# Another load order and a side-by-side start of block 1 in a matmul with logsumexp

## The chip, the core and the metric

The kernel runs on one core of one Trainium2 chip. The metric is the device time of one execution in microseconds; lower is better. The kernel before has a median of 441.1 us over 3 runs (440.34 to 441.67).

## The reference

```python
def setup_inputs():
    m, k, n = 1024, 4096, 4096
    return {"a": np.random.randn(m, k).astype(np.float32),
            "b": np.random.randn(k, n).astype(np.float32)}

def reference(a, b):
    x = np.matmul(a, b)
    return special.logsumexp(x, axis=-1).astype(np.float32)
```

The output is one number for each of the 1024 rows of A.

## The kernel before

**Tiling.** The rows of A form 8 tiles (`MT`, index `m`) of 128 rows, K is cut into 32 tiles (`KT`) of 128, and the columns of B into 8 blocks (`NB`, index `nb`) of 512. A and B lie in HBM as float32; the DMAs cast them to float16 on their way into SBUF. The row tiles go in four pairs or quads `q` (`m` = 2q and 2q+1), and the k tiles in 16 pairs (`KP`, index `i`), in four groups `g` of four pairs.

**Two ways to multiply.** Block 0 of the columns is done by plain matmuls (`plain`, L184; 128x512, 8 x 32 = 256 of them). Blocks 1 to 7 are done, quad by quad, by Strassen's scheme: seven products `m1` to `m7` of 16 matmuls of 128x256 each (all issued at L314) in place of eight. Their left operands are `aT` (A transposed), the sums `s1`, `s2`, `s5`, and `aT` after two differences were written into it in place; the right ones are raw blocks of B and `T1`, `T4`, `T6` and two in-place sums (`do_t1` to `do_t3`, on VectorE). A quad keeps two PSUM tiles `r0` = (c11, c12) and `r1` = (c21, c22). ScalarE copies intermediate states out (`s`, L359 and L364; `x`, L397 and L399), VectorE forms the sums (L78, L81) and the negated row maxima (`lse_max`, L84), and ScalarE the exponentials with their sums (`lse_exp`, L89); the exponentials of one quad are held in `pending` and issued by `flush` in the next.

**Load and transpose phase** (L139 to L281). K is taken in four chunks `kc` of 1024. A's part of a chunk comes as 8 DMAs (`load_a`, L155), one for each row tile, B's part of block 0 as 4 DMAs (L256), all from GpSimd's queue, each 256 KB as it lands. Each A load is staged in one of 12 slots, and a slot is used again for a later load. The slots lie in the memory that `T1`, `T4` and `T6` (tile `tb`) take later:

```python
    stg_slots = tb.rearrange("p t (i j) n -> p (t i) (j n)", j=4)
    NSLOT = 3 * KP // 4
        slot = stg_slots[:, (kc * MT + m) % NSLOT]
```

`transpose_group` (L160) transposes a staged tile with 8 matmuls (L166) into one of two PSUM tiles `tps_0`, `tps_1` in turn; groups of even number are copied to `aT` by VectorE (L177), odd ones by ScalarE (L179). The lists `arrivals` and `back` set the order: after the transposes of one arrival, TensorE does the work (`behind`) of the arrival two places earlier: the plain matmuls that became possible, and the sums of A (`a_sums_early`). Row tiles 6 and 7 have no PSUM tile in this phase, since six accumulators and the two `tps` take all eight banks; their plain matmuls come after the phase (L279 to L282), in the accumulators `acc_l`. Then VectorE prepares block 1 (L283 to L291), and the loop over blocks starts (L301).

**Warm-up matmuls.** `warm(n)` (L240) issues `n` matmuls of 128x512 on a zeroed region into the accumulator of row tile 5: ten before the loads, and three after each arrival until three A tiles of the first chunk have been through `behind`, 31 in all. The zeroed region is the last staging slot:

```python
    zeros = stg_slots[:, NSLOT - 1]
    nc.vector.memset(zeros[:, 0:FD], 0.0)
    warm(10)
```

**What sets the order.** `tc.manual_schedule()` keeps each engine's instructions in the order of the text. The waits between engines and DMAs are put in by the framework: each instruction waits for what stands before it in the text and writes what it reads, or reads or writes what it writes. In the loop of before, all loads of a chunk stand ahead of all transposes and warm-ups of that chunk, and behind those of the chunk before.

**PSUM and small buffers.** All PSUM tiles share one ring of 8 banks: six accumulators, two `tps`, then `acc_l` (the banks of row tiles 0 and 1), block 1's quad 0 (those of 2 and 3), quad 1 (4 and 5), quad 2 (`tps`), and so on. `s` and `x` have one buffer each. B's tiles `bt` have eight, four to a block.

Of the kernel before, what the change touches and what calls it, by code (L numbers as in the profile page):

```python
# [13 lines left out]
def kernel(  # L14
# [6 lines left out]
    nc = tc.nc  # L21
    P = 128
    FD = 512
    H = FD // 2
# [52 lines left out]
    def add(o, x, y):  # L77
        nc.vector.tensor_tensor(out=o, in0=x, in1=y, op=ALU.add)  # L78
# [71 lines left out]
        psum_pool.tile([P, 2 * FD], f16, name=f"tps_{h}", tag="ps") for h in range(2)  # L150
    ]

    def load_a(kc, m):
        slot = stg_slots[:, (kc * MT + m) % NSLOT]
        nc.gpsimd.dma_start(out=slot, in_=a_m[m, :, ts(kc, SC)])  # L155
        stg[kc, m] = slot

# [2 lines left out]
    def transpose_group(kc, m):  # L160
        src = stg.pop((kc, m))
        n = count[0]
        count[0] += 1
        pst = tps[n % 2]
        for j in range(JT):
            nc.tensor.matmul(  # L166
                pst[:, ts(j, P)],
                src[:, ts(j, P)],
                ident,
                is_transpose=True,  # L170
                start=(j == 0),
                stop=(j == JT - 1),
            )
        dst = aT[:, ts(kc, GI), :, m // 2, m % 2, :]
        v = pst.rearrange("p (i t c) -> p i t c", i=GI, t=2)
        if n % 2 == 0:
            nc.vector.tensor_copy(out=dst, in_=v)  # L177
        else:
            nc.scalar.copy(out=dst, in_=v)  # L179
# [3 lines left out]
    def plain(pt, i, kp, m):  # L183
        nc.tensor.matmul(  # L184
            pt,
            aT[:, i, kp, m // 2, m % 2, :],
            blk0.raw[i // GI][:, i % GI, kp, :],
            start=(done[m] == 0),
            stop=(done[m] == KT - 1),
        )  # L190
        done[m] += 1

    def a_sums_early(kc, q):
        r = ts(kc, GI)
        a11, a12 = aT[:, r, 0, q, 0, :], aT[:, r, 1, q, 0, :]
        a21, a22 = aT[:, r, 0, q, 1, :], aT[:, r, 1, q, 1, :]
        add(s1[:, r, q], a11, a22)
        add(s2[:, r, q], a21, a22)
        add(s5[:, r, q], a11, a12)

    def a_sums_late(q):
        a11, a12 = aT[:, :, 0, q, 0, :], aT[:, :, 1, q, 0, :]
        a21, a22 = aT[:, :, 0, q, 1, :], aT[:, :, 1, q, 1, :]
        sub(a21, a21, a11)
        sub(a12, a12, a22)

    def first_max(m):
        lse_max(acc[m // 2][m % 2], m, 0)
        lse_exp(acc[m // 2][m % 2], m, 0)


    arrivals = []
    for n, m in enumerate((0, 6, 1, 7, 2, 3, 4, 5)):
        arrivals.append(("a", m))
        if n < GI:
            arrivals.append(("b", n))

    have_a, have_b = [[] for _ in range(KC)], [[] for _ in range(KC)]

    def behind(kc, what, x):  # L220

        if what == "a":
            have_a[kc].append(x)
            todo = [(k, x) for k in have_b[kc]]
            if x % 2 == 1:
                a_sums_early(kc, x // 2)
        else:
            ks = [kc * JT + 2 * x, kc * JT + 2 * x + 1]
            have_b[kc].extend(ks)
            todo = [(k, m) for k in ks for m in have_a[kc]]  # L230
        for k, m in todo:
            if m < MT - 2:
                plain(acc[m // 2][m % 2], k // 2, k % 2, m)
        if kc == KC - 1 and what == "a" and x in (3, 4, 5):
            for m in {3: (0, 1), 4: (2,), 5: (3, 4, 5)}[x]:
                first_max(m)
            if x > 3:
                a_sums_late(x - 4)

    def warm(n):  # L240
        for _ in range(n):
            nc.tensor.matmul(acc[2][1], zeros[:, 0:P], zeros[:, 0:FD], start=True, stop=True)  # L242

    zeros = stg_slots[:, NSLOT - 1]
    nc.vector.memset(zeros[:, 0:FD], 0.0)  # L245
    warm(10)
    back = []
    for kc in range(KC):
        bt = bt_pool.tile([P, GI, 2, FD], f16, name=f"b_0_{kc}", tag="bt")
        blk0.raw.append(bt)  # L250
        for what, x in arrivals:
            if what == "a":
                load_a(kc, x)
            else:
                r0 = (kc * JT + 2 * x) * P
                nc.gpsimd.dma_start(  # L256
                    out=bt[:, x],
                    in_=b[r0 : r0 + 2 * P, ts(0, FD)].rearrange("(t p) n -> p t n", p=P),
                )
            if kc == 0 and x == 0 and what == "a":  # L260
                make_identity(nc, ident)
                nc.gpsimd.memset(negmax, 3.0e38)
                nc.gpsimd.memset(tsum, 0.0)
        for what, x in arrivals:
            if what == "a":
                transpose_group(kc, x)
            if kc == 0 and len(have_a[0]) < 3:
                warm(3)
            if len(back) == 2:
                behind(*back.pop(0))  # L270
            back.append((kc, what, x))
    while back:
        behind(*back.pop(0))

    blk = Block(1)
    for g in range(G):
        blk.raw.append(load_b(1, g))

    last = acc_tiles("l")  # L279
    for m in range(MT - 2, MT):  # L280
        for k in range(KT):  # L281
            plain(last[m % 2], k // 2, k % 2, m)  # L282
    for g in range(G):  # L283
        if g == G - 1:
            for m in range(MT - 2, MT):
                lse_max(last[m % 2], m, 0)
                lse_exp(last[m % 2], m, 0)
        for f in (blk.do_t1, blk.do_t6, blk.do_t4, blk.do_t7, blk.do_t3):
            f(g)
    for q in range(2, MP):  # L290
        a_sums_late(q)  # L291


    pending = []
# [6 lines left out]
    for nb in range(1, NB):  # L301
        nxt = None
        if nb + 1 < NB:
            nxt = Block(nb + 1)
            for g in range(G):
                nxt.raw.append(load_b(nb + 1, g))
        for q in range(MP):
            r0, r1 = acc_tiles(f"{nb}_{q}")
            c11, c12 = r0[:, 0:H], r0[:, H:FD]
            c21, c22 = r1[:, 0:H], r1[:, H:FD]  # L310

# [8 lines left out]
                        skip_group_check=True,  # L320
                    )

            first, tail = nb == 1 and q == 0, nxt is not None and q == MP - 1
            final = nxt is None and q == MP - 1

            s = fix_pool.tile([P, 3, H], f32, name=f"s_{nb}_{q}", tag="s")
            x = fix_pool.tile([P, 2, H], f32, name=f"x_{nb}_{q}", tag="x")

            def m1(c, **k):
                product(c, lambda i: s1[:, i, q], lambda i: T1[:, i], **k)  # L330

            def m5(c, **k):
                product(c, lambda i: s5[:, i, q], lambda i: blk.b(i, 1, 1), **k)

            def m2(c, **k):
                product(c, lambda i: s2[:, i, q], lambda i: blk.b(i, 0, 0), **k)

            def m6(c, **k):
                product(c, lambda i: aT[:, i, 0, q, 1], lambda i: T6[:, i], **k)

            def m7(c, **k):
                product(c, lambda i: aT[:, i, 1, q, 0], lambda i: blk.b(i, 1, 0), **k)
# [4 lines left out]
            def m4(c, **k):  # L347
                product(c, lambda i: aT[:, i, 1, q, 1], lambda i: T4[:, i], **k)

            if first:  # L350
                for g in range(G):
                    m1(c11, start=True, g=g)
                    m5(c12, g=g)
                    m2(c21, start=True, g=g)
                    m6(c22, g=g)
            else:
                m1(c11, start=True)
                m5(c12)
            nc.scalar.copy(out=s[:, 0:2], in_=r0.rearrange("p (h n) -> p h n", h=2))  # L359
            flush()  # L360
            if not first:
                m2(c21, start=True)
# [2 lines left out]
            if tail:  # L365
                for g in range(G):
                    nxt.do_t1(g)
            add(s[:, 2], s[:, 2], s[:, 1])
            sub(s[:, 0], s[:, 2], s[:, 0])
            if final:  # L370

                z = psum_pool.tile([P, FD], f32, name="z", tag="ps")[:, 0:H]
                y = fix_pool.tile([P, H], f32, name="y")
                m3(c12)
                nc.scalar.copy(out=x[:, 0], in_=c12)
                nc.scalar.copy(out=y, in_=c11)
                m4(c21)
                nc.scalar.copy(out=x[:, 1], in_=c21)
                m7(z, start=True)
                sub(x[:, 0], x[:, 0], s[:, 0])  # L380
                sub(y, y, s[:, 2])
                lse_max(c12, 2 * q, nb)
                lse_exp(c12, 2 * q, nb)
                add(c22, c22, x[:, 0])
                lse_max(r1, 2 * q + 1, nb)
                lse_exp(r1, 2 * q + 1, nb)
                add(y, y, x[:, 1])
                add(z, z, y)
                lse_max(z, 2 * q, NB)
                lse_exp(z, 2 * q, NB)  # L390
                continue
# [12 lines left out]
            for h in range(2):  # L404
                lse_max(rows[h], 2 * q + h, nb)
                pending.append(lambda h=h, q=q, nb=nb, rows=rows: lse_exp(rows[h], 2 * q + h, nb))
            if tail:
                for f in (nxt.do_t4, nxt.do_t7, nxt.do_t3):
                    for g in range(G):
                        f(g)  # L410
# [43 lines left out]
```

## Time and profile before

| | |
|---|---|
| median of 3 runs | 441.1 us |
| the profiled execution | 441.06 us, of which the span from first to last instruction is 438.6 us |
| TensorE busy | 427.2 us (97%), 3679 matmuls |
| VectorE, ScalarE, GpSimd busy | 228.1 us (52%), 109.7 us (25%), 54.1 us (12%) |
| mean granted TensorE clock | 0.997 |
| read from HBM | 83.89 MB |
| A loads / loads of B's block 0 | 32 / 16 DMAs of 256 KB, some 9.5 us from issue to landing |
| loads of B's blocks 1 to 7 | 4 DMAs of 1024 KB each |

The times of the profile count from the first instruction. In the answers below, a line of the timeline has the start, the length, the engine, the line of the kernel, the operation, what it writes and reads, the count, and in brackets how long the engine was idle before it and what released it. Instructions of one kind in a row are merged to one line. A matmul's length reaches over the next one's start, so the pace of matmuls is read from the starts.

### The profile page before, as it was taken

The page shows a single profiled execution, that of the slowest core. Times are in us where ns is not written, and L with a number is a line of the kernel's source. Part 1 is how long each engine was busy: PE and PEld are TensorE (multiplying, and loading weights), DVE is VectorE, ACT ScalarE, POOL GpSimd, SP SyncE. Part 2 cuts the span into 40 slices and gives each one's busy share as a digit, 9 for nine tenths or more (in the row PEclk, how much of TensorE's full clock was granted, in tenths as well). Part 3 has the DMA queues.
Part 4 walks back from the last instruction along what each step waited for, and adds up shares of the span by engine and source line. Part 5 has one row for each costly group of instructions (what it writes and reads, how often), then busy time and mean ns, then how long its engine had stood idle before and what let it go on. Part 6 is the DMA issues. An engine that isn't in the chain of part 4 may idle for free.

```text
span 438.6 us, 8381 instructions
## 1 busy us (share of the span) xinstructions
PE 427.2 (97%) x3679; PEld 348.9 (80%) x3679; DVE 228.1 (52%) x425; ACT 109.7 (25%) x262; POOL 54.1 (12%) x84
## 2 busy tenths in 40 slices
PE   7999999999999999999999999999999999999995
PEld 3555554488888888888888888888888888888884
DVE  0434449973358632693348732693347722693224
ACT  2122324012222212222222122222222122222223
POOL 7435440200003000300003000300003000000000
PEclk9999999999999999999999999999999999999998
DMA  8999999998008920298008920199007930000000
GB/s 128 208 207 207 209 208 207 207 207 136 2 0 137 207 44 0 31 207 149 1 0 130 207 50 1 24 207 157 0 1 122 208 57 0 2 1 1 1 1 0
DMA packets 38260, 42.48 MB, mean 97 GB/s; under 512 B 1360, under 2 KB 34128, under 8 KB 38224
## 3 DMA queue, kind: packets, MB, share of 16 engines
q0 software_dynamic: 38080, 41.95, 56.9%
q8 instruction: 28, 0.46, 0.4%
q14 instruction: 8, 0.07, 0.1%
q1 hardware_dynamic: 144, 0.00, 0.0%
HBM read 83.89 MB, written 0.00 MB: 191 GB/s over the span
## 4 chain that ended last, share of the span: by engine, by line
PE 85%; DMA 11%; POOL 2%; issue 1%; DVE 1%; ACT 0%; POOLq 0%; DVEq 0%
DMA tb<-in_a_dram 6%; DMA b_3_540<-in_b_dram 2%; DMA b_2_395<-in_b_dram 2%; PE acc_0_0_2460 L314 2%; PE acc_0_0_1916 L314 2%; PE acc_0_0_4084 L314 2%; PE acc_0_0_3004 L314 2%; PE acc_0_0_1372 L314 2%; PE acc_0_0_3548 L314 2%; PE acc_1_0_3677 L314 2%; PE acc_3_0_2847 L314 2%; PE acc_2_0_1086 L314 2%; PE acc_3_0_3391 L314 2%; PE acc_2_0_3262 L314 2%; PE acc_1_0_2589 L314 2%; PE acc_3_0_1759 L314 2%
## 5 line engine op out<-in xcount | busy, mean ns | idle before, releaser
L314 PEld LDWEIGHTS <-aT 128*128 128x128 f16 x1792 | 175.2, 98 | 24.3 <-issue 4.2
L314 PEld LDWEIGHTS <-s_69 128*128 128x128 f16 x448 | 43.8, 98 | 5.3
L314 PEld LDWEIGHTS <-s_70 128*128 128x128 f16 x448 | 43.8, 98 | 5.1
L314 PEld LDWEIGHTS <-s_71 128*128 128x128 f16 x448 | 43.8, 98 | 5.1
L184 PEld LDWEIGHTS <-aT 128*128 128x128 f16 x256 | 24.0, 98 | 24.6
L177 DVE COPY aT<-tps_84 128x1024 f16<-128x1024 f16 x16 | 11.1, 692 | 39.8 <-PE tps_84 L166 39.8
L179 ACT COPY aT<-tps_85 128x1024 f16<-128x1024 f16 x16 | 16.2, 1012 | 50.8 <-PE tps_85 L166 50.8
L166 PEld LDWEIGHTS <-tb 128*128 128x128 f16 x256 | 16.2, 99 | 14.7 <-DMA tb<-in_a_dram 11.1
L155 POOL DMA_DIRECT2D tb<-in_a_dram x32 | 17.7, 555 | 26.0 <-PE tps_84 L166 11.6
L166 PE MATMUL tps_85<-ident,tb 128*128 128x128 f16 x128 | 9.9, 220 | 3.8 <-DMA tb<-in_a_dram 3.6
L166 PE MATMUL tps_84<-ident,tb 128*128 128x128 f16 x128 | 10.1, 224 | 1.0 <-DMA tb<-in_a_dram 1.0
L242 PE MATMUL acc_1_83<-tb 128*128 128x512 f16 x31 | 9.6, 461 | 1.2 <-DVE tb L245 1.2
L81 DVE TENSOR_TENSOR aT<-aT 128x2048 f16<-128x2048 f16 x8 | 9.3, 1222 | 0.0
L242 PEld LDWEIGHTS <-tb 128*128 128x128 f16 x31 | 3.2, 112 | 4.9 <-issue 2.2
L78 DVE TENSOR_TENSOR s_69<-aT 128x512 f16<-128x512 f16 x16 | 6.7, 418 | 0.1
L78 DVE TENSOR_TENSOR s_71<-aT 128x512 f16<-128x512 f16 x16 | 6.7, 420 | 0.0
L78 DVE TENSOR_TENSOR s_70<-aT 128x512 f16<-128x512 f16 x16 | 6.7, 419 | 0.0
L104 POOL DMA_DIRECT2D b_0_2452<-in_b_dram x1 | 0.9, 878 | 46.1 <-PE acc_3_0_2303 L314 46.1
L104 POOL DMA_DIRECT2D b_0_3540<-in_b_dram x1 | 0.9, 878 | 46.1 <-PE acc_3_0_3391 L314 46.1
L104 POOL DMA_DIRECT2D b_0_1908<-in_b_dram x1 | 0.9, 878 | 46.0 <-PE acc_3_0_1759 L314 46.0
L104 POOL DMA_DIRECT2D b_0_2996<-in_b_dram x1 | 0.9, 878 | 46.0 <-PE acc_3_0_2847 L314 46.0
L104 POOL DMA_DIRECT2D b_0_1364<-in_b_dram x1 | 0.9, 873 | 43.7 <-PE acc_3_0_1215 L314 43.7
(1034 smaller groups left out, 844.7 us busy)
## 6 DMA issues: line engine op xcount, KB each, us to landing
tb<-in_a_dram POOLq DMA_DIRECT2D x32, 256.0 KB, 9.5
b_0_97<-in_b_dram POOLq DMA_DIRECT2D x4, 256.0 KB, 7.1
b_1_250<-in_b_dram POOLq DMA_DIRECT2D x4, 256.0 KB, 9.2
b_2_395<-in_b_dram POOLq DMA_DIRECT2D x4, 256.0 KB, 9.3
b_3_540<-in_b_dram POOLq DMA_DIRECT2D x4, 256.0 KB, 9.3
b_0_720<-in_b_dram POOLq DMA_DIRECT2D x1, 1024.0 KB, 13.6
b_1_722<-in_b_dram POOLq DMA_DIRECT2D x1, 1024.0 KB, 17.4
b_2_724<-in_b_dram POOLq DMA_DIRECT2D x1, 1024.0 KB, 21.2
```

The costliest lines, as they stand in the source:

```text
L78: nc.vector.tensor_tensor(out=o, in0=x, in1=y, op=ALU.add)
L81: nc.vector.tensor_tensor(out=o, in0=x, in1=y, op=ALU.subtract)
L104: nc.gpsimd.dma_start(out=flat[:, h * step : (h + 1) * step], in_=rows[:, g * 2 * GI + h * step : g * 2 * GI + (h + 1) * step, ts(nb, FD)],)
L155: nc.gpsimd.dma_start(out=slot, in_=a_m[m, :, ts(kc, SC)])
L166: nc.tensor.matmul(pst[:, ts(j, P)], src[:, ts(j, P)], ident, is_transpose=True, start=(j == 0), stop=(j == JT - 1),)
L177: nc.vector.tensor_copy(out=dst, in_=v)
L179: nc.scalar.copy(out=dst, in_=v)
L184: nc.tensor.matmul(pt, aT[:, i, kp, m // 2, m % 2, :], blk0.raw[i // GI][:, i % GI, kp, :], start=(done[m] == 0), stop=(done[m] == KT - 1),)
L242: nc.tensor.matmul(acc[2][1], zeros[:, 0:P], zeros[:, 0:FD], start=True, stop=True)
L314: nc.tensor.matmul(c, lhs(i), rhs(i), start=(start and i == 0), stop=(i == KP - 1), skip_group_check=True,)
```

## The change

- **Load order.** `arrivals` becomes one list over all chunks: for each chunk the A tiles 0 to 5 with the four pieces of B's block 0 between them, and behind the last chunk the A tiles 6 and 7 of all four chunks. The slot of a load is its number in this list modulo 12.
- **Where the loads stand in the text.** Ahead of each arrival's transposes, as many loads are issued as there are slots: an A load while fewer than 12 A loads are ahead of the transposes, a B load always. Block 1's loads follow the last of them.
- **Plain matmuls of tiles 6 and 7** run as these tiles arrive; `acc_l` is taken when the first of them does.
- **Sums of A.** `a_sums_late` is done by chunk for quads 0 to 2; those of quad 3, early and late, move behind quad 1 of block 1. `first_max` of row tiles 0 to 5 moves with the arrivals; that of 6 and 7 moves from the fourth to the third group of block 1's preparation.
- **Quads 0 and 1 of block 1** are issued side by side: for each group `g`, the pieces of `m1`, `m5`, `m2`, `m6` of quad 0 and then of quad 1. The other three products follow quad by quad.
- **Small buffers.** `s` and `x` become one tile of four parts, in which `x` takes parts 1 and 3; the copy of `r0` is called `e` and lies in parts 0 and 1 of `s`, but in a tile of its own in quad 1 of block 1 and in the last quad (where it also takes over from `y`).

```diff
+    loads = [0]
     def load_a(kc, m):
-        slot = stg_slots[:, (kc * MT + m) % NSLOT]
+        slot = stg_slots[:, loads[0] % NSLOT]
+        loads[0] += 1
...
-    for n, m in enumerate((0, 6, 1, 7, 2, 3, 4, 5)):
-        arrivals.append(("a", m))
-        if n < GI:
-            arrivals.append(("b", n))
+    for kc in range(KC):
+        for m in range(MT - 2):
+            arrivals.append((kc, "a", m))
+            if m < GI:
+                arrivals.append((kc, "b", m))
+    for kc in range(KC):
+        for m in range(MT - 2, MT):
+            arrivals.append((kc, "a", m))
...
         for k, m in todo:
-            if m < MT - 2:
-                plain(acc[m // 2][m % 2], k // 2, k % 2, m)
-        if kc == KC - 1 and what == "a" and x in (3, 4, 5):
-            for m in {3: (0, 1), 4: (2,), 5: (3, 4, 5)}[x]:
-                first_max(m)
-            if x > 3:
-                a_sums_late(x - 4)
+            if m == MT - 2 and k == 0:
+                acc.append(acc_tiles("l"))
+            plain(acc[m // 2][m % 2], k // 2, k % 2, m)
+        if what == "a" and x % 2 == 1 and x < MT - 2:
+            a_sums_early(ts(kc, GI), x // 2)
+        if kc > 0 and what == "a" and x in (3, 4, 5):
+            a_sums_late(ts(kc - 1, GI), x - 3)
+        if kc == KC - 1 and what == "a" and x in (4, 5):
+            first_max(2 * x - 8)
+            first_max(2 * x - 7)
+        if what == "a" and x >= MT - 2:
+            n = 2 * kc + x - (MT - 2)
+            if n < 2:
+                first_max(4 + n)
+            elif n < 5:
+                a_sums_late(ts(KC - 1, GI), n - 2)
...
     zeros = stg_slots[:, NSLOT - 1]
     nc.vector.memset(zeros[:, 0:FD], 0.0)
     warm(10)
...
+    coming = list(arrivals)
     back = []
...
+    for kc, what, x in arrivals:
+        while coming and (coming[0][1] == "b" or loads[0] < count[0] + NSLOT):
+            load(*coming.pop(0))
+            if loads[0] == 1 and not blk0.raw:
                 make_identity(nc, ident)
                 nc.gpsimd.memset(negmax, 3.0e38)
                 nc.gpsimd.memset(tsum, 0.0)
...
+        if not coming and not blk.raw:
+            for g in range(G):
+                blk.raw.append(load_b(1, g))
+        if what == "a":
+            transpose_group(kc, x)
+        if kc == 0 and len(have_a[0]) < 3:
+            warm(3)
+        if len(back) == 2:
+            behind(*back.pop(0))
+        back.append((kc, what, x))
...
-    for m in range(MT - 2, MT):
-        for k in range(KT):
-            plain(last[m % 2], k // 2, k % 2, m)
-    for g in range(G):
-        if g == G - 1:
+        if g == 2:
             for m in range(MT - 2, MT):
-                lse_max(last[m % 2], m, 0)
-                lse_exp(last[m % 2], m, 0)
+                first_max(m)
...
-            s = fix_pool.tile([P, 3, H], f32, name=f"s_{nb}_{q}", tag="s")
-            x = fix_pool.tile([P, 2, H], f32, name=f"x_{nb}_{q}", tag="x")
+            s = fix_pool.tile([P, 4, H], f32, name=f"s_{nb}_{q}", tag="s")
+            x, e = s[:, 1::2], s[:, 0:2]
+            if final or (first and q == 1):
+                e = fix_pool.tile([P, 2, H], f32, name=f"e_{nb}_{q}", tag="e")
...
-            if first:
+            if first and q == 0:
                 for g in range(G):
-                    m1(c11, start=True, g=g)
-                    m5(c12, g=g)
-                    m2(c21, start=True, g=g)
-                    m6(c22, g=g)
-            else:
+                    for p in both:
+                        u0, u1 = quads[p]
+                        m1(u0[:, 0:H], p=p, start=True, g=g)
+                        m5(u0[:, H:FD], p=p, g=g)
+                        m2(u1[:, 0:H], p=p, start=True, g=g)
+                        m6(u1[:, H:FD], p=p, g=g)
+            elif not first:
                 m1(c11, start=True)
                 m5(c12)
-            nc.scalar.copy(out=s[:, 0:2], in_=r0.rearrange("p (h n) -> p h n", h=2))
+            nc.scalar.copy(out=e, in_=r0.rearrange("p (h n) -> p h n", h=2))
             flush()
...
+            if first and q == 1:
+                a_sums_early(slice(0, KP), MP - 1)
+                a_sums_late(slice(0, KP), MP - 1)
```

More of the change, by code (lines that the diff above doesn't have):

```diff
@@ L191, in plain, with a_sums_early @@
         done[m] += 1
-    def a_sums_early(kc, q):
-        r = ts(kc, GI)
+    def a_sums_early(r, q):
         a11, a12 = aT[:, r, 0, q, 0, :], aT[:, r, 1, q, 0, :]
@@ L199, in a_sums_early, with a_sums_late @@
         add(s5[:, r, q], a11, a12)
-    def a_sums_late(q):
-        a11, a12 = aT[:, :, 0, q, 0, :], aT[:, :, 1, q, 0, :]
-        a21, a22 = aT[:, :, 0, q, 1, :], aT[:, :, 1, q, 1, :]
+    def a_sums_late(r, q):
+        a11, a12 = aT[:, r, 0, q, 0, :], aT[:, r, 1, q, 0, :]
+        a21, a22 = aT[:, r, 0, q, 1, :], aT[:, r, 1, q, 1, :]
         sub(a21, a21, a11)
@@ L224, in behind @@
             todo = [(k, x) for k in have_b[kc]]
-            if x % 2 == 1:
-                a_sums_early(kc, x // 2)
         else:
@@ L246, with load @@
     warm(10)
-    back = []
[L248 to L253, printed above, removed]
-            else:
[L255 to L260, printed above, removed]
+    blk = Block(1)
+    def load(kc, what, x):
+        if what == "a":
+            load_a(kc, x)
+            return
+        if x == 0:
+            blk0.raw.append(bt_pool.tile([P, GI, 2, FD], f16, name=f"b_0_{kc}", tag="bt"))
+        r0 = (kc * JT + 2 * x) * P
+        nc.gpsimd.dma_start(
+            out=blk0.raw[kc][:, x],
+            in_=b[r0 : r0 + 2 * P, ts(0, FD)].rearrange("(t p) n -> p t n", p=P),
+        )
+    coming = list(arrivals)
+    back = []
+    for kc, what, x in arrivals:
+        while coming and (coming[0][1] == "b" or loads[0] < count[0] + NSLOT):
+            load(*coming.pop(0))
+            if loads[0] == 1 and not blk0.raw:
                 make_identity(nc, ident)
@@ L263 @@
                 nc.gpsimd.memset(tsum, 0.0)
[L264 to L271, printed above, removed]
+        if not coming and not blk.raw:
+            for g in range(G):
+                blk.raw.append(load_b(1, g))
+        if what == "a":
+            transpose_group(kc, x)
[4 more added lines that the diff above has]
+        back.append((kc, what, x))
     while back:
         behind(*back.pop(0))
-    blk = Block(1)
     for g in range(G):
-        blk.raw.append(load_b(1, g))
-    last = acc_tiles("l")
-    for m in range(MT - 2, MT):
-        for k in range(KT):
-            plain(last[m % 2], k // 2, k % 2, m)
-    for g in range(G):
-        if g == G - 1:
+        if g == 2:
             for m in range(MT - 2, MT):
-                lse_max(last[m % 2], m, 0)
-                lse_exp(last[m % 2], m, 0)
+                first_max(m)
         for f in (blk.do_t1, blk.do_t6, blk.do_t4, blk.do_t7, blk.do_t3):
             f(g)
-    for q in range(2, MP):
-        a_sums_late(q)
     pending = []
@@ L306 @@
                 nxt.raw.append(load_b(nb + 1, g))
+        quads = {}
         for q in range(MP):
-            r0, r1 = acc_tiles(f"{nb}_{q}")
+            if q not in quads:
+                both = (0, 1) if nb == 1 and q == 0 else (q,)
+                for p in both:
+                    quads[p] = acc_tiles(f"{nb}_{p}")
+            r0, r1 = quads[q]
             c11, c12 = r0[:, 0:H], r0[:, H:FD]
@@ L321, in product, with m1, m5, m2 @@
                     )
-            first, tail = nb == 1 and q == 0, nxt is not None and q == MP - 1
+            first, tail = nb == 1 and q < 2, nxt is not None and q == MP - 1
             final = nxt is None and q == MP - 1
-            s = fix_pool.tile([P, 3, H], f32, name=f"s_{nb}_{q}", tag="s")
-            x = fix_pool.tile([P, 2, H], f32, name=f"x_{nb}_{q}", tag="x")
[L329 to L339, printed above, removed]
+            s = fix_pool.tile([P, 4, H], f32, name=f"s_{nb}_{q}", tag="s")
+            x, e = s[:, 1::2], s[:, 0:2]
+            if final or (first and q == 1):
+                e = fix_pool.tile([P, 2, H], f32, name=f"e_{nb}_{q}", tag="e")
+            def m1(c, p=q, **k):
+                product(c, lambda i: s1[:, i, p], lambda i: T1[:, i], **k)
+            def m5(c, p=q, **k):
+                product(c, lambda i: s5[:, i, p], lambda i: blk.b(i, 1, 1), **k)
+            def m2(c, p=q, **k):
+                product(c, lambda i: s2[:, i, p], lambda i: blk.b(i, 0, 0), **k)
+            def m6(c, p=q, **k):
+                product(c, lambda i: aT[:, i, 0, p, 1], lambda i: T6[:, i], **k)
             def m7(c, **k):
@@ L348, in m4 @@
                 product(c, lambda i: aT[:, i, 1, q, 1], lambda i: T4[:, i], **k)
-            if first:
+            if first and q == 0:
                 for g in range(G):
-                    m1(c11, start=True, g=g)
-                    m5(c12, g=g)
-                    m2(c21, start=True, g=g)
-                    m6(c22, g=g)
-            else:
+                    for p in both:
+                        u0, u1 = quads[p]
[4 more added lines that the diff above has]
+            elif not first:
                 m1(c11, start=True)
                 m5(c12)
-            nc.scalar.copy(out=s[:, 0:2], in_=r0.rearrange("p (h n) -> p h n", h=2))
+            nc.scalar.copy(out=e, in_=r0.rearrange("p (h n) -> p h n", h=2))
             flush()
@@ L367 @@
                     nxt.do_t1(g)
-            add(s[:, 2], s[:, 2], s[:, 1])
-            sub(s[:, 0], s[:, 2], s[:, 0])
+            add(s[:, 2], s[:, 2], e[:, 1])
+            sub(s[:, 0], s[:, 2], e[:, 0])
             if final:
                 z = psum_pool.tile([P, FD], f32, name="z", tag="ps")[:, 0:H]
-                y = fix_pool.tile([P, H], f32, name="y")
+                y = e[:, 0]
                 m3(c12)
```

## The prediction, made before the changed kernel was run

> **What bounds the kernel now.** The page first: its slices of TensorE and of DMA traffic.
>
> ```profile
> PE   7999999999999999999999999999999999999995
> ...
> GB/s 128 208 207 207 209 208 207 207 207 136 2 0 137 207 44 0 31 207 149 1 0 130 207 50 1 24 207 157 0 1 122 208 57 0 2 1 1 1 1 0
> ```
>
> A slice is 11 us. The DMAs run flat out at some 207 GB/s for the first eight slices and have gaps from then on; TensorE is busy nearly throughout. So two limits meet before 88 us, and only one holds afterwards. The chain that ended last shows where they part (start, length, what):
>
> ```profile
> 53.80 10.02 DMA tb<-in_a_dram
> 63.87 0.62 PE tps_85 L166 x8
> ...
> 73.15 6.91 PE acc_l_728 L184 x32
> 80.06 6.91 PE acc_l_729 L184 x32
> 86.96 0.87 PE acc_0_0_830 L314 x8
> ...
> 99.19 3.49 PE acc_1_0_957 L314 x32
> ```
>
> Up to 63.9 us a DMA is on the chain; from there to 431.5 us, matmul follows matmul. The time is therefore the moment at which block 1's first product starts (86.80 by its row in the timeline) plus products that never wait: 109 ns each (3.49 / 32). Whatever moves that start moves the end. The timeline shows how the load phase spends its time:
>
> ```profile
> 1.19 4.45 PE L242 MATMUL acc_1_83<-tb 128*128 128x512 f16 x10 [1.19 <-DVE tb L245]
> ...
> 5.43 0.95 PE L166 MATMUL tps_84<-ident,tb 128*128 128x128 f16 x8
> ...
> 6.22 1.46 PE L242 MATMUL acc_1_83<-tb 128*128 128x512 f16 x6
> ...
> 8.83 0.62 PE L166 MATMUL tps_85<-ident,tb 128*128 128x128 f16 x8 [1.15 <-DMA tb<-in_a_dram]
> ...
> 17.89 0.55 POOL L155 DMA_DIRECT2D tb<-in_a_dram  x1 [4.05 <-PE tps_84 L166]
> ...
> 17.93 0.62 PE L166 MATMUL tps_85<-ident,tb 128*128 128x128 f16 x8 [0.34 <-DMA tb<-in_a_dram]
> ...
> 24.10 1.09 POOL L155 DMA_DIRECT2D tb<-in_a_dram  x2 [1.63 <-DMA b_1_250<-in_b_dram]
> ...
> 32.03 0.62 PE L166 MATMUL tps_84<-ident,tb 128*128 128x128 f16 x8 [0.18 <-DMA tb<-in_a_dram]
> ...
> 33.28 0.62 PE L166 MATMUL tps_85<-ident,tb 128*128 128x128 f16 x8 [0.63 <-DMA tb<-in_a_dram]
> ```
>
> Three things are to be seen. Transposes wait for their DMA (8.83, 17.93, 32.03, 33.28): arrivals 3, 10, 21 and 22 of the queue, so one arrival takes (33.28 - 17.93) / 12 = 1.28 us. A staged slot is waited for by itself: the load at 17.89 waited for the transposes of the tile that had its slot, and the warm-ups at 1.19 waited for the memset of the last slot, while those at 6.22 ran with loads into three other slots under way. And the load into the last slot, which the warm-ups read, is by the order of the text in the pair at 24.10, nine us after the last warm-up ended.
>
> **The change, part by part.** *Load order alone.* Count TensorE's load-phase work by starts: a transpose group 0.436 us (65.63 - 65.19 holds one), a plain matmul 0.216 (6.91 / 32), a warm-up 0.2165. A chunk of before holds 8 groups and 48 plain matmuls, 13.9 us, against 12 arrivals or 15.3 us: TensorE waits in each. The new chunk holds 6 groups and 48 matmuls, 2.62 + 10.37 = 13.0 us, against 10 arrivals, 12.8 us. Walking the new list (each start is the later of the previous end and the landing; the same walk on the old list gives 86.75 where 86.80 was measured), TensorE meets its last wait for data at 11.6 us, at A tile 2. Behind that it has 9 warm-ups, 30 groups and 254 plain matmuls, 1.95 + 13.08 + 54.84 = 69.9 us, so it would end them at 81.5. One wait is new: A tile 1 of chunks 1 to 3 is copied by ScalarE, and its plain matmuls come 0.436 + 0.43 + 0.436 = 1.30 us after its transposes start, while the copy starts 0.66 after that and takes 1.01: some 0.1 for two semaphores more, and 0.5 us is lost, three times. (0 to 0.8 each; ScalarE is idle 50.8 us in all before its 16 copies, so no queue is added.) That makes 83.0.
>
> *Warm-ups and slots: the deciding part.* Ahead of the first arrival's transposes the new loop issues 12 A loads, numbers 0 to 11, and eight B loads. Number 11 (tile 5 of chunk 1, the 20th arrival) goes into slot 11, the region that all warm-ups read. The ten early ones stand before this in the text, but the 21 others now stand behind it, and so they wait for that DMA, as the transposes at 8.83 wait for theirs. The 20th arrival lands at 17.93 + 10 x 1.28 = 30.7; I take 30.8 with the semaphore. It can't be held up itself: its slot's ten readers end at 5.4, and the 19 loads ahead of it need no slot that is in use.
>
> TensorE's first warm-up stands behind A tile 0's transposes, and everything else behind it. At 30.8 it still has 21 warm-ups (4.55), 31 groups (13.52) and 256 plain matmuls (55.27): 73.3 us, to 104.1 at full pace, since 20 arrivals are then in SBUF. Two terms are added. The three ScalarE waits, 1.5. And the pace after a pause of 24.6 us: at its first start TensorE took 0.43 us for a warm-up against 0.2165 later, and 0.79 for the first group against 0.436, which lost 10 x 0.214 + 0.35 = 2.5 us. The longest pause of the load phase before (1.15 us) did not bring this back, so the bounds are 0 and 2.5; 24.6 us is much nearer to the state at the start, and I take 2.5. The start of block 1 is then 104.1 + 1.5 + 2.5 = 108.1, against 86.8: **+21.3 us**.
>
> The Trainium skill, "TensorE: Matmul & The Clock Gate", section "What's actually happening", says that the gate halves the clock after an idle window of about 3.4 us and opens it after about 3.4 us of work. By that page the term would be 1.7 us, and the forecast below 0.8 us lower. Before, no pause of TensorE behind its start was as long, so the trace of before can't show whether that holds.
>
> *Who is held by the wait.* ScalarE and VectorE have only copies of groups that are not there. GpSimd's queue stops at load 13, whose slot 1 is free after A tile 1's transposes, at 30.8 + 2.6 for six warm-ups at half pace + 0.9 = 34.3; arrivals 21 and 22 land till 33.3, and the next some 3.6 us after its issue, so DMA loses 5 us. This is covered: a load is 12 groups ahead of its use. The last A load is free at the transposes of load 19, 29.9 us before the end of plain work, 78.2; it lands about 82, and block 1's four pieces at 5.07 us each (1024 KB at 207 GB/s) by 103. The fourth is wanted at 108.1 + 3 x 3.49 = 118.6: 15 us of cover. Block 2's loads go into block 0's buffers, free at the last plain matmuls, 49 us ahead of their use.
>
> *Side by side.* The matmuls are the same. A group's worth of work is 32 x 0.109 = 3.49 us, on data long there. VectorE's preparation starts behind the last copy on its queue, some 4 us before block 1, and takes 3.2 us for a group and 1.3 for two maxima: the last `T6` is ready at about 116, 2.7 us ahead of need. What is added is a handover. Quad 1's `m7` adds to c11, which ScalarE must have copied out, and this copy now stands behind quad 0's last `x` copy. Before, quad 0's last product ended at 99.03 by the next start; the `x` copy ran from 99.23, the next copy would start 0.27 later (as 429.72 to 429.99) and take 0.59: `m7` can start at 100.13, 1.1 us late. Then `m4` wants c21 copied, behind two exponentials that wait for maxima ending at 101.92 and 102.51: copy done near 103.8, `m4` due at 103.6. Together **+1.3 us** (0.9 to 1.7).
>
> *At nothing.* `a_sums` in other pieces: VectorE has 26.1 us of them against 25.5, and is idle half the time; quad 3's 5.9 us run during quad 2, 12.2 us ahead of use. Maxima and exponentials of tiles 0 and 1 free `acc_l`'s banks some 3 us after A tile 6 arrives, and it is wanted 4.3 after. `x` over `e`: the `x` copy must now follow the sum that reads `e` (ends 146.7, copy at 147.03 in the tightest quad), and the next `e` copy must follow c22's sum (137.5 against 139.40); if either cover went, ScalarE would be late by tenths, off TensorE's path.
>
> Sum: 441.06 + 21.3 + 1.3 = **463.7 us** (the profiled execution stands at the median of 441.1). Its own range takes in 0 for the clock term, 0 to 0.8 three times, 0.9 to 1.7: 459 to 465.
>
> **The rivals.** *No such wait (438.6).* If the warm-ups are not held by load 11, because that load goes out behind them after all or because they are not tied to it, block 1 starts at 83.0, 3.8 earlier, less the handover of 1.3: 441.06 - 2.5. For it speaks that TensorE's waits for data in the load phase are real and removed by the order. Against it: every reader of a staged slot in the trace waits for the last writer, the memset included. It decides from the point where the first warm-up after A tile 0 ends before 10 us; the wait costs more than the 3.8 gained if it lasts beyond about 11 us. That the change doesn't do what it says is this case too.
>
> *The feed runs dry (468).* If the loads, held to the pace of freed slots, lose more than the 15 us of cover, block 1's groups are waited for, microsecond for microsecond; with its 20.3 us of transfer taking twice that, the fourth group is 5 us late. Against it: the DMAs move 207 GB/s whenever something is queued.
>
> **How the numbers follow.** The held warm-ups 0.87, no wait 0.08, dry feed 0.05. The range 459.5 to 466 leaves out the second and third and little of the first. A measurement of this kernel can tell 0.3%, 1.3 us, from no change: faster 0.08, same 0.01, slower 0.91.
>
> **What would show it.** Right: the warm-up line L242 with one idle stretch of about 24 us released by a DMA into `tb`, ending near 30.8; matmuls of 0.43 us spacing behind it; DMA traffic falling around 34 to 38; the first L314 product near 108; a TensorE wait of about a microsecond for ScalarE before quad 1's `m7`; and no other wait to the end. Wrong: warm-ups done by 16 us, or TensorE waiting for `in_a_dram` after 31 us or for block 1's pieces.

## The result, and the profile after

The changed kernel takes 462.64 us (median of 4 runs, 462.36 to 464.31); the kernel before, run beside it, 441.24. The ratio is 1.050, 95% interval 1.047 to 1.053. The forecast was 463.7 us, in a range of 459.5 to 466.0. The profiled execution took 462.89 us, its span 461.1, against 441.06 and 438.6 before: the span grew by 22.5 us, and 22.6 were forecast.

The slices of the page, now 11.5 us each: TensorE, its granted clock in tenths, and DMA.

```profile
PE   4039999999999999999999999999999999999995
PEclk8559999999999999999999999999999999999999
GB/s 129 208 163 144 149 179 106 202 207 207 134 1 2 62 207 99 1 8 203 157 1 0 149 207 12 1 83 207 77 1 24 206 136 1 2 1 1 0 1 1
```

TensorE is nearly idle in the second slice and most of the third, in which its clock is granted by half; the DMAs run flat out in the second slice and then drop below 180 GB/s until the eighth. Before, neither row had such a hole. The waits of TensorE, all that the view lists for the whole span (in total, times, longest):

```profile
PE acc_1_83 L257 <- DMA tb<-in_a_dram: 24.3, 1, 24.3
PE acc_1_83 L257 <- DVE tb L260: 1.2, 1, 1.2
PE acc_1_0_836 L332 <- ACT e_1_1027 L382: 0.9, 1, 0.9
PE acc_1_79 L187 <- ACT aT L182: 0.7, 3, 0.2
```

L257 is the warm-up matmul (L242 before), and `tb` the memory of the staging slots: one warm-up waited 24.3 us for a load of A. There is no other wait for data; before, the transposes had ten of them. The chain that ended last, at the places where it matters:

```profile
20.81 9.55 DMA tb<-in_a_dram
...
30.40 2.74 PE acc_1_83 L257 x6
33.14 0.85 PE tps_85 L169 x8
34.00 2.46 PE acc_1_83 L257 x6
...
108.25 0.87 PE acc_0_0_834 L332 x8
...
127.50 0.37 ACT s_0_838 L422
127.87 0.50 ACT e_1_1027 L382
...
128.41 3.65 PE acc_1_0_836 L332 x32
```

The load issued at 20.81 lands at 30.36 and lets the warm-ups go; six of them and a transpose group take twice their time, block 1 starts at 108.1 (its row in the timeline begins at 108.09), and quad 1's `m7` stands behind two ScalarE copies. From 128.4 on the chain is matmuls to the end, as before.

### The profile page after: what moved, and what is told of

Its sections match the earlier page's. It is cut to its first block, busy times and chain, and to the rows that moved or that the text cites. A ratio compares the mean times of both kernels' runs of the same rounds, so it can differ in the third digit from the quotient of the medians.

```text
span 461.1 us, 8378 instructions
## 1 busy us (share of the span) xinstructions
PE 428.5 (93%) x3679; PEld 350.5 (76%) x3679; DVE 228.2 (49%) x434; ACT 109.6 (24%) x262; POOL 54.2 (12%) x84
## 4 chain that ended last, share of the span: by engine, by line
PE 91%; DMA 6%; ACT 1%; DVE 1%; POOL 1%; issue 0%; POOLq 0%; DVEq 0%
DMA b_1_115<-in_b_dram 2%; DMA tb<-in_a_dram 2%; PE acc_0_0_2458 L332 2%; PE acc_0_0_2998 L332 2%; PE acc_0_0_4070 L332 2%; PE acc_0_0_3538 L332 2%; PE acc_0_0_1378 L332 2%; PE acc_0_0_1918 L332 2%; PE tps_85 L169 2%; PE acc_1_79 L187 2%; PE acc_1_0_836 L332 2%; PE acc_1_83 L257 2%; PE acc_2_0_3254 L332 2%; PE acc_1_0_2046 L332 2%; PE acc_0_0_834 L332 2%; PE acc_2_0_4326 L332 2%
## 5 line engine op out<-in xcount | busy, mean ns | idle before, releaser
L257 PE MATMUL acc_1_83<-tb 128*128 128x512 f16 x31 | 12.3, 555 | 25.5 <-DMA tb<-in_a_dram 24.3
L257 PEld LDWEIGHTS <-tb 128*128 128x128 f16 x31 | 3.7, 130 | 30.7 <-DMA tb<-in_a_dram 24.5
L169 PEld LDWEIGHTS <-tb 128*128 128x128 f16 x256 | 17.4, 100 | 8.2 <-issue 0.6
L81 DVE TENSOR_TENSOR aT<-aT 128x512 f16<-128x512 f16 (+1 forms) x26 | 11.3, 480 | 0.0
L78 DVE TENSOR_TENSOR s_70<-aT 128x512 f16<-128x512 f16 (+1 forms) x13 | 6.2, 480 | 0.0
L78 DVE TENSOR_TENSOR s_71<-aT 128x512 f16<-128x512 f16 (+1 forms) x13 | 6.2, 480 | 0.0
L78 DVE TENSOR_TENSOR s_69<-aT 128x512 f16<-128x512 f16 (+1 forms) x13 | 6.2, 478 | 0.0
```

The source lines that it names most:

```text
L81: nc.vector.tensor_tensor(out=o, in0=x, in1=y, op=ALU.subtract)
L169: nc.tensor.matmul(pst[:, ts(j, P)], src[:, ts(j, P)], ident, is_transpose=True, start=(j == 0), stop=(j == JT - 1),)
```

## The experiments

Theory: the warm-ups read slot 11, the 12th A load now overwrites it ahead of them, and nearly the whole loss is the wait for its landing, with the half pace behind it. Rival: the new order itself, or loads held to the pace of freed slots, costs the time. For the small terms of the sum there are experiments of their own.

**Zeros where no load goes.**

```diff
-    zeros = stg_slots[:, NSLOT - 1]
+    zeros = aT[:, KP - 1, 1].rearrange("p q h c -> p (q h c)")
```

> The changed kernel, with the warm-ups' zeros in a part of aT that nothing writes before chunk 3, so that no staged load overwrites what they read. Theory (the held warm-ups are the whole loss): the pause of 24 us goes, block 1 starts at 81.5 + 1.2 (three ScalarE waits as measured, 0.4 each) = 82.7 against 86.8 of the kernel before, the handover of quad 1 stays at 1.26, and the time is 441.1 - 4.1 + 1.3 = 438.3 us (437 to 440). Rival (the new order itself, or loads at the pace of freed slots, costs the time): TensorE still waits for data and the time stays over 445 us.

Measured: 438.12 us (6 runs, 437.25 to 439.06), and 438.16 (12 runs) when it was run again beside two later kernels: ratios to the kernel before 0.993 (0.992 to 0.995) and 0.995 (0.994 to 0.997). The repeat ranged from 437.75 to 440.44. One line takes away 24.5 us and turns the change from 5% slower to 0.5 to 0.7% faster. The waits of this kernel that stand in the place of those above:

```profile
PE tps L169 <- DMA tb<-in_a_dram: 2.5, 2, 2.4
...
PE acc L332 <- ACT e L382: 0.9, 1, 0.9
PE acc L187 <- ACT aT L182: 0.7, 3, 0.2
```

TensorE waits for data twice, at A tiles 1 and 2, and not after 12.7 us; the three waits for ScalarE's copies and the handover are those of the changed kernel. Block 1 starts at 84.04 in this execution, where 82.7 was expected, since A tile 1 was there only at 10.13 us; in the profiled execution of the repeat it was there at 8.91, and block 1 starts at 82.81.

**The same zeros in an earlier slot of the changed kernel** (slot 8: the 15th arrival).

```diff
-    zeros = stg_slots[:, NSLOT - 1]
+    zeros = stg_slots[:, 8]
```

> The changed kernel with the warm-ups' zeros in slot 8 in place of slot 11. Slot 8 is loaded with tile 2 of chunk 1, the 15th arrival in place of the 20th. Theory: the warm-ups are let go at its landing, five arrivals of 1.28 us earlier, at 30.4 - 6.4 = 24.0 us, and everything behind is earlier by as much: 462.6 - 6.4 = 456.2 us (455.4 to 457.0). Rival (the pause has another cause than this one load): 462.6 us.

Measured: 456.18 us (455.89 to 456.60), ratio 1.035 (1.034 to 1.037). TensorE's wait is 18.4 us and ends at 24.54. Five arrivals earlier are 5.9 us by the release and 6.5 by the time, of which 0.4 is a half pace that cost less here (2.5 us in place of 2.9): the time follows the landing of the load that the warm-ups' memory receives.

**The wait alone, in the order of before.**

```diff
-    zeros = stg_slots[:, NSLOT - 1]
+    zeros = stg_slots[:, 5]
```

This edit is made in the kernel before.

> The kernel before, old order and all, with the warm-ups' zeros in slot 5 in place of slot 11. Slot 5 is loaded with tile 5 of chunk 0, the 12th arrival, which stands ahead of the 21 later warm-ups in the text. Theory: they wait for its landing at 17.93 + 2 x 1.28 = 20.5 us; then 73.3 us of work and 2.85 us of half pace (as the changed kernel lost) end at 96.7 against 86.8, so 441.1 + 9.9 = 451.0 us (449.5 to 452.5). Rival (the loss belongs to the new order or to its loads): 441 us.

Measured: 452.49 us (452.31 to 452.67), ratio 1.026 (1.025 to 1.028), at the upper end of what was expected. The old order pays for such a wait too, so the rival falls. Block 1 starts at 99.0, 2.3 us later than expected, though, and the timeline says why:

```profile
20.06 2.74 PE L242 MATMUL acc<-tb 128*128 128x512 f16 x6 [13.57 <-DMA tb<-in_a_dram]
...
45.51 0.55 POOL L155 DMA_DIRECT2D tb<-in_a_dram  x1 [4.62 <-PE tps L166]
...
76.08 0.62 PE L166 MATMUL tps<-ident,tb 128*128 128x128 f16 x8 [0.63 <-DMA tb<-in_a_dram]
```

Loads that wait for slots fall behind, and here TensorE waits for data again, up to the last tiles, at 76.1 us where it was 63.9 before. The feed runs dry, as in the forecast's third case, though at the tiles of A and not at block 1's pieces. These waits cost some 3 us by the starts (2.1 in the wait list, five times), and the 2.3 are what is left of them after a release 0.4 us earlier and a half pace 0.8 us cheaper than expected. In the new order, with its loads issued as slots come free, the changed kernel has no such wait.

**TensorE kept busy in the pause** (112 matmuls on zeros in `aT`, whose result is overwritten later).

```diff
+    own = aT[:, KP - 1, 1].rearrange("p q h c -> p (q h c)")[:, 0:FD]
+    nc.vector.memset(own, 0.0)
...
+        if (kc, what, x) == (0, "a", 0):
+            for _ in range(112):
+                nc.tensor.matmul(acc[2][1], own[:, 0:P], own, start=True, stop=True)
         if kc == 0 and len(have_a[0]) < 3:
             warm(3)
```

> The changed kernel, its 21 warm-ups held as they are, with 112 more matmuls of 128x512 on other zeros (in aT) between A tile 0's transposes and the first held warm-up, 24.2 us at full pace, so that TensorE does not stand idle in the pause. Theory: the release at 30.4 stays, the half pace behind it goes (12 warm-ups and one group took 5.89 us where 3.03 are due, 2.85 lost): 462.6 - 2.85 = 459.8 us (459.2 to 460.4). By the 3.4 us window of the Trainium skill, page TensorE: Matmul & The Clock Gate, it would be 1.7 us: 460.9. Rival (the slow stretch comes from the wait, not from TensorE having been idle): 462.6 us.

Measured: 460.76 us (460.40 to 461.15), 1.9 us below the changed kernel, outside the expected range and near the 460.9 of the one window.

```profile
5.92 24.34 PE L294 MATMUL acc<-aT 128*128 128x512 f16 x112
31.15 1.47 PE L257 MATMUL acc<-tb 128*128 128x512 f16 x6 [0.89 <-DMA tb<-in_a_dram]
32.45 0.61 PE L169 MATMUL tps<-ident,tb 128*128 128x128 f16 x8
```

Six held warm-ups now take 1.30 us by the starts, not 2.74. So the half pace came from TensorE's idleness, and its whole term is gone (12 warm-ups and a group: 31.15 to 34.20, 3.05 us, the 3.03 due). So the nearness to 460.9 is chance: the release was 0.75 us later in this execution, and the two profiled executions differ by 2.1 us, which is 2.85 less 0.75. Whether the matmuls had a part in the later release is open; the slot 8 kernel, which has none of them, issues its 12th A load at 21.05 us, against 20.81 in the changed kernel and 21.21 here.

**Quads 0 and 1 one by one** (with the zeros in `aT`).

```diff
-                both = (0, 1) if nb == 1 and q == 0 else (q,)
+                both = (q,)
...
-            first, tail = nb == 1 and q < 2, nxt is not None and q == MP - 1
+            first, tail = nb == 1 and q == 0, nxt is not None and q == MP - 1
...
-            if first and q == 1:
+            if nb == 1 and q == 1:
                 a_sums_early(slice(0, KP), MP - 1)
...
```

> The first of these kernels (zeros in aT) without the side-by-side part: quad 0 of block 1 in pieces as before, then quad 1 by itself. Theory: the handover (1.26 us) goes, but quad 0 alone uses a group in 1.75 us, and VectorE has T1 of groups 2 and 3 ready only at 86.7 and 89.9 us, where 86.2 and 88.5 are due: 1.9 us of waits. Net + 0.6 us: 438.9 (437.8 to 440). Rival A (block 1's groups are all there in time): 437.0. Rival B (the side-by-side part saves more than the two terms): over 440.

Measured: 436.56 us (436.28 to 436.82), ratio 0.990 (0.989 to 0.991): 1.6 us faster than side by side, where I expected 0.6 slower.

```profile
76.94 1.28 DVE L78 TENSOR_TENSOR tb<-b 128x1024 f16<-128x1024 f16 x2
...
82.82 0.60 PE L332 MATMUL acc<-tb,s 128*128 128x256 f16 x4
...
87.54 1.29 DVE L78 TENSOR_TENSOR tb<-b 128x1024 f16<-128x1024 f16 x2
...
88.28 0.60 PE L332 MATMUL acc<-tb,s 128*128 128x256 f16 x4
```

The fourth group starts 5.46 us behind the first, 0.2 more than three groups take (5.24): VectorE had started on block 1 at 76.9, some 6 us ahead of its first product and not the 4 of the forecast, and was ahead. So rival A holds but for 0.2 us, and at this start of block 1 the side-by-side part costs the handover of 1.26 for those 0.2. The profiled execution of the repeat above, with the same start of block 1 (82.81), took 437.79 us against 436.82 here, which is this 1.0 us; the other 0.6 of the medians is not placed.

**A tile 1 copied by VectorE** (on top of the last).

```diff
-        if n % 2 == 0:
+        if n % 2 == 0 or m == 1:
             nc.vector.tensor_copy(out=dst, in_=v)
```

> Zeros in aT and quads one by one (436.6 us), and A tile 1 of every chunk copied out of its PSUM tile by VectorE too (0.69 us) in place of ScalarE (1.01). Theory: the three waits of TensorE for ScalarE, 0.4 each, shrink to under 0.1: 436.6 - 1.0 = 435.6 us (435.1 to 436.1), with the L187 row's waits for ScalarE's L182 gone. Rival (those waits are made good later by waits for data): 436.6.

Measured: 436.35 us (435.98 to 436.80), ratio 0.990. The waits for ScalarE are gone from the list, block 1 starts at 81.83, 1.0 us earlier, and the profiled span is 1.0 shorter (433.8 against 434.8). A tile 2, the last wait for data, came at the same moment in both (11.41 and 11.45), so the 1.0 us lies behind it. The spans of all four executions are shorter too (433.8 to 434.1 against 434.4 to 434.9), but the median moved by 0.2 only: the two kernels ran on different chips, and the executions had 1.7 to 2.0 us outside the span there and 2.0 to 2.7 here. The step is shown in the trace and not in the time.

**Fewer warm-ups** (on top of the last).

```diff
-        if kc == 0 and len(have_a[0]) < 3:
+        if kc == 0 and len(have_a[0]) < 2:
```

> The same as the kernel with A tile 1 copied by VectorE, with warm-ups only until two A tiles have been through behind: 15 after the loads in place of 21. Theory: the last six stand where TensorE no longer waits for data, so most of their 1.30 us is on the path (the walk over the arrivals gives 1.15): 435.6 - 1.1 = 434.5 us (434.0 to 435.2). Rival (TensorE falls back to half pace in the longer gaps): over 436.

Measured: 436.34 us (435.54 to 437.10), the same as without the edit. Neither theory nor rival: no half pace came, but a new wait did.

```profile
87.15 1.29 DVE L78 TENSOR_TENSOR tb<-b 128x1024 f16<-128x1024 f16 x2 [1.01 <-DMA b<-in_b_dram]
87.90 0.60 PE L332 MATMUL acc<-tb,s 128*128 128x256 f16 x4 [1.16 <-DVE tb L78]
```

From A tile 2's transposes to block 1 it took 69.2 us, against 70.4 in the kernel before it, so the six warm-ups did go off the path; A tile 2 came 0.7 us later in this execution (12.10 against 11.41), and block 1 starts at 81.33, 0.5 earlier. But block 1's fourth piece lands at 87.1, and TensorE waits for the sum of it: with quads one by one the landing has become the bound, and a quicker TensorE gains nothing.

**The first copy of the handover early** (side by side, zeros in `aT`).

```diff
+            if final or (first and q == 0):
+                e2 = fix_pool.tile([P, 2, H], f32, name=f"e_{nb}_{q}", tag="e")
             if final or (first and q == 1):
-                e = fix_pool.tile([P, 2, H], f32, name=f"e_{nb}_{q}", tag="e")
+                e = e2
...
-            nc.scalar.copy(out=e, in_=r0.rearrange("p (h n) -> p h n", h=2))
+            if not (first and q == 1):
+                nc.scalar.copy(out=e, in_=r0.rearrange("p (h n) -> p h n", h=2))
...
             nc.scalar.copy(out=s[:, 2], in_=c21)
+            if first and q == 0:
+                nc.scalar.copy(out=e2, in_=quads[1][0].rearrange("p (h n) -> p h n", h=2))
```

> Zeros in aT with quads 0 and 1 side by side (438.1 us), and ScalarE copies quad 1's c11 and c12 out right after quad 0's c21, ahead of quad 0's x copies. Theory: the handover wait of 1.1 us before quad 1's m7 goes: 438.1 - 1.1 = 437.0 us (436.4 to 437.7), no TensorE wait for the copy into e. Rival (side by side costs what it costs by something else): 438.1, the same as without the edit.

Measured: 438.12 us (437.42 to 440.20), the same.

```profile
106.60 0.37 ACT L390 COPY s<-acc 128x256 f32<-128x256 f32 x1
...
107.02 1.91 PE L332 MATMUL acc<-tb,aT 128*128 128x256 f16 x16 [1.09 <-ACT s L390]
```

The wait before `m7` is gone, and `m4` waits 1.09 us for the copy of c21, which stands behind quad 0's exponentials: the second wait of the handover was bound to the maxima, not to the first wait.

**Both copies early.** In quad 1 `flush` moves behind the copy of c21.

```diff
-            flush()
+            if not (first and q == 1):
+                flush()
...
             nc.scalar.copy(out=s[:, 2], in_=c21)
+            if first and q == 1:
+                flush()
...
```

> As the kernel with the early copy of quad 1's c11 and c12, and in quad 1 ScalarE also copies c21 ahead of the two exponentials of quad 0, which it did behind them. Theory (the handover has two waits in a row, and the early copy alone only brought the second one forward: 1.09 us before quad 1's m4, released by the copy of c21): both go, 1.26 us less than with side by side as it was: 438.1 - 1.3 = 436.8 us (436.2 to 437.6), no TensorE wait for ScalarE behind block 1's start. Rival (the handover costs the same by a third wait): 438.1.

Measured: 436.64 us (435.98 to 437.40), ratio 0.991 (0.989 to 0.992); the kernel with the zeros in `aT` alone, beside it on the same chip, 438.16: 1.5 us less. TensorE has no wait behind block 1's start.

**All together:** zeros in `aT`, side by side with both copies early, A tile 1 copied by VectorE, fewer warm-ups, each by the edit shown above.

> Side by side with both copies early, zeros in aT, A tile 1 copied by VectorE, 15 warm-ups behind the loads. Theory: with quads one by one the kernel of these edits waits 1.33 us for the preparation of block 1's fourth piece (87.90 where 86.57 was due), since that piece lands at 87.1; side by side it is due 5.2 us later, so this wait goes: 436.3 - 1.3 = 435.0 us (434.3 to 435.8). Rival (side by side has no use): 436.3.

Measured: 434.54 us (434.15 to 434.80), ratio 0.986 (0.984 to 0.987), the fastest kernel of the study. All its waits of TensorE:

```profile
PE acc L257 <- DVE aT L260: 1.2, 1, 1.2
PE tps L169 <- DMA tb<-in_a_dram: 0.8, 2, 0.6
```

Block 1 starts at 80.86, and TensorE no longer waits for the fourth piece (VectorE still does, 0.96 us). Here side by side earns its place: 1.8 us against the one-by-one kernel with the same other edits (436.34). By the profiled executions 1.33 of it is that kernel's wait for the fourth piece; the other 0.5 is the earlier start of block 1 (81.33 there), where A tile 2 came 0.7 us earlier here, and is not the side-by-side part's.

The repeat of the first experiment, for the two kernels above:

> The changed kernel with the zeros in aT once more, beside the other two on one chip: 438.1 us (437.2 to 438.8), with the handover of 1.1 + 0.15 us.

It gave the 438.16 us already told.

## Why the prediction was right

*The deciding step held.* The held warm-ups were read off the text of the loop (12 loads ahead of the first warm-up, number 11 into the memory that they read) and off two rows of the trace: readers wait for the last writer of their slot, and the 20th arrival lands near 30.7. It landed at 30.4. Two kernels that tie the zeros to another load (slot 8, and slot 5 in the old order) and one that takes them out of every load's way show that the time follows this landing.

*The sum to block 1's start* was 108.1 and came out at 108.1, with terms that were off and cancelled. The release was 0.4 earlier. The half pace cost 2.85 us, not 2.5: twelve warm-ups and a group took 30.40 to 36.29, where 3.03 us are due. The three waits for ScalarE's copies were 0.4 each, 1.2 in all, not 1.5 (52.54 is the start of the first held matmul, 52.14 was due). The rest of the work took 0.3 us more than by my rates. That the sum came out to a tenth of a microsecond is luck.

The half pace is where the Trainium skill was weighed ("TensorE: Matmul & The Clock Gate", "What's actually happening"). The windows view of the changed kernel has it in the granted clock (0.51, the third number from the end):

```profile
30.40:36.30 5.90, 5.90 (x21) 2.65 (x22) 0.00 (x0) 1.01 (x1) 1.25 (x2) 0.51 0.49 68
```

The same twelve warm-ups and group took 5.89 us here and 5.49 and 5.10 behind the shorter pauses of the slot experiments, so 2.9, 2.5 and 2.1 us were lost. The 2.9 lies outside the bounds that the prediction gave this term, 0 and 2.5, and all three lie above the 1.7 of one 3.4 us window. The row of the kernel's own start, 2.5, came near, but one such row is a draw from a spread: the same start lost 1.65 us in one execution of the kernel with its own zeros and 2.5 in another (the rows are in the last section). The page also says that the window runs freely; a full window of work could then end up to two windows after work begins, an estimate from that page with which 2.9 lost would agree. That idleness brings the half pace, as the page says, is what the busy pause shows.

*Nothing else waited,* as forecast: DMA ran at 94 GB/s from 31 to 40 us while loads waited for slots, and no group of block 1 was late. VectorE's last `T6` was ready at 114.1, 1.9 us earlier than I had it.

*The handover* was 1.26 us (0.9 in the wait list, 1.11 by the starts before `m7`, 0.15 before `m4`), forecast 1.3. What I had not seen is that its two waits are tied: the second is the floor, and the experiment on the first alone gained nothing.

*The rival without the wait* was priced at 438.6; the kernel with the zeros elsewhere took 438.1. *The miss of 1.1 us* against the median lies mostly outside the span: 1.8 us of the profiled execution lay there, against 2.5 before, and I had carried the 2.5 over.

## What to carry to other kernels

A helper that borrows a buffer (here zeros in the last staging slot) is part of that buffer's order: before loads are hoisted, look up every later reader of every slot that they fill, also those whose values don't matter, since a wait is put in for them all the same. Scratch operands belong in memory that is written late, and a load that runs ahead by all slots leaves none for them. When a wait is removed and the time stays, look one wait further on the same path: the copy, the landing or the exponential that was just behind it.

## What was not expected of the hardware

The half pace cost 2.1 us after a pause of 13.6 us, 2.5 after 18.4 and 2.9 after 24.3, by the starts of the warm-ups. The pause's length need not be the reason. The kernel with the zeros in `aT` was profiled twice, and in both executions its first warm-up starts at 1.19 us:

```profile
5.43 1.05 PE L169 MATMUL tps<-ident,tb 128*128 128x128 f16 x8
...
6.29 1.49 PE L257 MATMUL acc<-aT 128*128 128x512 f16 x6
```

```profile
4.98 0.62 PE L169 MATMUL tps<-ident,tb 128*128 128x128 f16 x8
...
5.44 1.46 PE L257 MATMUL acc<-aT 128*128 128x512 f16 x6
```

Ten warm-ups and a group, 2.60 us at full pace, are over at 6.29 in the first and at 5.44 in the repeat: 2.5 and 1.65 us lost by the same instructions. Over the starts of all kernels with these zeros it was 1.5 (one by one) to 2.9 us (all together), as wide as behind the three pauses; what sets it within that is open. A pause of 2.35 us, ahead of A tile 1 in the first of these executions, did not bring the half pace back: the six warm-ups behind it took 1.46 us again.

The view gives a granted clock of 1.00 for the first 5 us of the kernel before, though its first ten warm-ups ran at 0.43 us each; so at the start of a trace the pace of the matmuls says more than that column. A tile 1's transposes started at 10.13 us in one execution of the kernel with its own zeros and at 8.91 in another, and block 1 moved by 1.2 us with them; what holds that landing back is open.
